# Moving half of the conditioning steps out of the top-16 search into the expert loop and the feed-forward part

## The chip, the core and the metric

The kernel runs on one core of a Trainium2 chip. The core has five engines that each run a queue of their own in order: TensorE (PE) for matmuls, VectorE (DVE), ScalarE (ACT), GpSimd (POOL) and SyncE (SP), which here only issues transfers. Engines wait for each other through semaphores, and transfers between DRAM and the core's SBUF run on 16 DMA engines beside them. The metric is the device time of one execution in microseconds (us). Three runs of the kernel before gave 2368.1, 2367.86 and 2363.62 us: a median of 2367.86 us.

## The reference, cut to what matters

The program is two blocks one after the other on 512 tokens of width 1024. The first is a gated delta rule with a pooling branch, then a product-key mixture of 16,384 experts (eight heads, top 16 of each). The second block is an attention mixer and a feed-forward part, both modulated by six vectors that depend on nothing but a small input `c`. These six vectors are what the text calls the conditioning.

```python
# first block: experts
q = (xb @ w_query).reshape(t, 8, 2, 128)
scores = jnp.einsum("thpc,hpkc->thpk", q, sk)
s1, i1 = lax.top_k(scores[:, :, 0], 16)
s2, i2 = lax.top_k(scores[:, :, 1], 16)
cand = (s1[..., :, None] + s2[..., None, :]).reshape(t, 8, 256)
top_s, top_pos = lax.top_k(cand, 16)
gate = jax.nn.softmax(top_s, axis=-1)
act = gelu(jnp.einsum("td,thkd->thk", xb, expert_down[idx]))
x = x + jnp.einsum("thk,thkd->td", gate * act, expert_up[idx])
...
# second block
mod_all = jnp.einsum('bd,lde->lbe', silu(c), ada_w) + ada_b[:, None]
sh_m, sc_m, gt_m, sh_f, sc_f, gt_f = jnp.split(mod_all[0], 6, axis=-1)
h = modulate(rms_norm(x, norm_g[0, 0]), sh_m, sc_m)
y = stick_breaking_mixer(h, sb_w_qkv, sb_w_o)
x = x + gt_m * rms_norm(y, norm_g[0, 1])
h = modulate(rms_norm(x, norm_g[0, 2]), sh_f, sc_f)
y = swiglu_ffn(h, ffn_w_in, ffn_w_out)
x = x + gt_f * rms_norm(y, norm_g[0, 3])
```

`sh_f` and `sc_f` are first needed in the second block, after attention; `gt_f` is needed at the very end.

## The kernel before, in words

Every matmul is done as three passes on a high and a low part of both factors (`mm3`, lines 198 to 200), so each weight block goes through `split` (line 170): a load of 512 KB into a tile `raw` (SP, line 178), the high part by ACT (`uh` or `wh`, line 187), the low part by DVE or POOL (`ul` or `wl`, line 188). The tiles `raw` share a ring of four buffers for the whole program. SP issues in the order of the program as it is built, so a load whose buffer is not yet free holds back every transfer that SP has behind it. A scheduler that simulates the program sets each engine's order and gives each tile a fixed buffer; both are settled when the program is built.

The stages follow each other in the profiled execution about so (us from the span's start): first mixer 0 to 230, delta rule to 355, output product to 384, search to 539, decoding of the found indices to 612, gates to 877, a tail of expert-down tiles to 925, expert loop to 1675, attention to 1990, output product and feed-forward part to 2365.

The search (from line 1000): for each of 16 half heads a query product with a weight tile (`query`), scores `S`, and the top 16 by DVE (`top16`, lines 980 to 985); after two half heads the 53 candidates `C` (lines 1031 to 1038). The first token block of 128 is done by a gathered path (its rows fetched by POOL's indirect DMA, line 936); the other three, 384 tokens, do all 16,384 experts densely with gates that are zero for those not chosen. An expert-down tile of 128 experts is 24 matmuls of 384 columns and a gelu by ACT (line 975); an expert-up tile is 18 matmuls of 512 columns (three blocks, two halves, three passes). The first 74 down tiles are computed ahead of the loop as fillers (`fill`) and stored to DRAM (`acts`): `FILL_QUERY` of them in the search, others in the delta rule's later part, the decoding and the gates, and the rest of the 74 after the gates (`self.fill(SPILL)`, line 855). The loop over 128 tiles (variable `n`) takes groups of four, one group loading its four stored activations, the next computing them. It multiplies them by the gates (line 882), splits them into `ah` (883) and `al` (884), loads and splits the up tile, and runs the up product two tiles later (`LOOK`). Six of the eight PSUM banks hold its sums.

The conditioning is a generator, `ada` (line 1149), advanced by `ada_steps`. For each of six vectors: eight steps that load 512 KB of `ada_w` into a `raw` tile (1164), scale it by ACT (1165) and add it by POOL (1167); then one step that takes three more `raw` tiles at once, `row` (the bias, loaded from DRAM), `hi` and `lo` (the two parts of the sum, lines 1173 and 1174), runs four matmuls with a matrix of ones and adds the result to `row` (1180); then one step for the finish (a product on POOL and a sum, or for a gate vector a product and a store to DRAM). Thirty steps run in the delta rule and thirty, two after each half head, in the search.

## Time and profile before

| | |
|---|---|
| median of three runs | 2367.86 us |
| profiled execution | 2367.24 us |
| its span on the core | 2365.4 us (1.84 us lie around it) |
| mean granted TensorE clock | 0.979 of full speed |
| PE, DVE, ACT, POOL busy | 95%, 71%, 40%, 37% |
| DMA | 467.90 MB, mean 198 GB/s |

The busy share is an average over stages with different limits; the table of stages among the rows below is read first, then for one stage what each engine waited for. "A <- B" in a table of waits means that A stood idle until B ended. A wait on SP's queue is the time in which a transfer could not be issued.

### The profile page before, as it was taken

To read this page: it belongs to the slowest core of one execution; us is meant where nothing else is said; L and a number is where in the kernel's file an instruction comes from. 1 tells how busy PE (TensorE), PEld (TensorE's weight loads), DVE (VectorE), ACT (ScalarE), POOL (GpSimd) and SP (SyncE) were. 2 spreads that over 40 slices of the span, in tenths; PEclk is the share of its full clock that TensorE was granted. 3 is DMA by queue.
4 is the path that set the end of the run, shared out by engine and by line. 5 is a ranking of instruction groups with operands and counts; after the bars stand their busy time and mean duration, and the time that the engine had idled before them with its cause. 6 is when DMAs were issued, how large, how long until landed. Compare 5 with 4: busy or idle time off the path is not lost.

```text
span 2365.4 us, 31745 instructions
## 1 busy us (share of the span) xinstructions
PE 2245.3 (95%) x11953; PEld 1911.1 (81%) x11953; DVE 1668.4 (71%) x2761; ACT 955.0 (40%) x1422; POOL 885.7 (37%) x553
## 2 busy tenths in 40 slices
PE   7898998887999999999999999999899999999998
PEld 6678767777999999888888888888787667888887
DVE  6675536899999975777878888888747766333334
ACT  4454325444344443433333333333446665322222
POOL 4367414773122112655555656565213331000000
PEclk9899999998999999999999999999999999999999
DMA  4223214455789878899999999999231122322221
GB/s 169 80 73 128 76 63 152 163 196 176 249 321 318 310 276 284 308 316 322 327 320 334 333 323 320 324 323 318 97 99 45 45 83 91 120 98 90 92 85 63
DMA packets 179850, 467.90 MB, mean 198 GB/s; under 512 B 15344, under 2 KB 83952, under 8 KB 178032
## 3 DMA queue, kind: packets, MB, share of 16 engines
q1 hardware_dynamic: 141824, 329.33, 40.4%
q0 software_dynamic: 36864, 134.23, 16.0%
q10 hardware_dynamic: 1008, 2.31, 0.3%
q8 instruction: 93, 1.52, 0.3%
q14 instruction: 61, 0.50, 0.1%
HBM read 420.86 MB, written 44.96 MB: 197 GB/s over the span
## 4 chain that ended last, share of the span: by engine, by line
PE 67%; DVE 14%; DMA 7%; issue 5%; ACT 4%; POOL 3%; SPq 0%; DVEq 0%; ACTq 0%; POOLq 0%
PE bank L198 19%; PE bank L200 19%; PE bank L199 19%; PE bank L1364 3%; PE bank L1137 3%; PE bank L653 3%; DMA act<-acts 2%; DMA raw<-in_e_down_dram 2%; DVE ul L188 2%; DVE su L949 1%; DVE cy L470 1%; DMA raw<-in_ada_w_dram 1%; ACT uh L187 1%; DVE x L955 1%; POOL ada_acc L1167 1%
## 5 line engine op out<-in xcount | busy, mean ns | idle before, releaser
L198 PE MATMUL bank<-actT_h,wh 128*128 128x384 f32 (+2 forms) x1672 | 597.4, 358 | 23.9 <-ACT wh L187 12.2
L200 PE MATMUL bank<-actT_h,wl 128*128 128x384 f32 (+2 forms) x1672 | 587.7, 354 | 14.2 <-POOL wl L188 10.5
L199 PE MATMUL bank<-actT_l,wh 128*128 128x384 f32 (+2 forms) x1672 | 590.0, 353 | 1.6 <-DVE actT_l L331 1.2
L187 ACT ACTIVATE wh<-raw 128x1024 fp32r<-128x1024 f32 x190 | 201.1, 1059 | 418.3 <-PE bank L199 261.5
L198 PEld LDWEIGHTS bank<-actT_h,wh 128*128 128x128 f32 x1672 | 318.2, 190 | 52.3 <-ACT wh L187 15.8
L200 PEld LDWEIGHTS bank<-actT_h,wl 128*128 128x128 f32 x1672 | 317.4, 190 | 40.3 <-POOL wl L188 13.8
L199 PEld LDWEIGHTS bank<-actT_l,wh 128*128 128x128 f32 x1672 | 318.0, 190 | 25.2 <-DVE actT_l L331 1.4
L187 ACT ACTIVATE uh<-raw 128x1024 fp32r<-128x1024 f32 x194 | 202.8, 1052 | 301.1 <-PE bank L200 150.9
L199 PE MATMUL bank<-ul,ah 128*128 128x512 f32 x768 | 303.3, 395 | 0.0
L198 PE MATMUL bank<-uh,ah 128*128 128x512 f32 x768 | 303.0, 395 | 0.0
L200 PE MATMUL bank<-uh,al 128*128 128x512 f32 x768 | 302.0, 395 | 0.8 <-DVE al L884 0.8
L188 POOL TENSOR_TENSOR wl<-raw,wh 128x1024 fp32r<-128x1024 f32 x89 | 224.6, 2525 | 163.6 <-ACT wh L187 79.9
L188 DVE TENSOR_TENSOR ul<-raw,uh 128x1024 fp32r<-128x1024 f32 x167 | 225.9, 1356 | 78.3 <-ACT uh L187 77.6
L936 POOL DMA_INDIRECT su<-in_e_up_dram,rows_of x128 | 191.2, 1493 | 174.1 <-DVE x L955 152.4
L188 DVE TENSOR_TENSOR wl<-raw,wh 128x1024 fp32r<-128x1024 f32 x115 | 140.4, 1222 | 112.6 <-ACT wh L187 111.3
L260 POOL TENSOR_TENSOR rs<-ms,nhalf 128x1 f32<-128x1 f32 (+1 forms) x23 | 16.0, 696 | 458.9 <-DVE ms L259 458.9
L955 DVE SCALAR_TENSOR_TENSOR x<-su,own_act,x 128x1024 f32<-128x1024 f32 x128 | 178.4, 1394 | 1.1
L200 PEld LDWEIGHTS bank<-uh,al 128*128 128x128 f32 x768 | 144.2, 188 | 36.1 <-DVE al L884 1.5
L199 PEld LDWEIGHTS bank<-ul,ah 128*128 128x128 f32 x768 | 144.2, 188 | 32.7
L198 PEld LDWEIGHTS bank<-uh,ah 128*128 128x128 f32 x768 | 144.2, 188 | 32.2
L936 POOL DMA_INDIRECT su<-in_e_rows_dram,rows_of x76 | 110.5, 1454 | 128.1 <-DVE su L949 74.5
L882 DVE TENSOR_TENSOR act<-act,G 128x384 f32<-128x384 f32 x128 | 89.9, 715 | 67.3 <-DMA act<-acts 40.2
(397 smaller groups left out, 3834.2 us busy)
## 6 DMA issues: line engine op xcount, KB each, us to landing
raw<-in_e_down_dram SPq DMA_DIRECT2D x128, 512.0 KB
raw<-in_e_up_dram SPq DMA_DIRECT2D x128, 512.0 KB
raw<-in_ada_w_dram SPq DMA_DIRECT2D x48, 512.0 KB
gates<-stg SPq DMA_DIRECT2D x12, 2048.0 KB
G<-gates SPq DMA_DIRECT2D x32, 768.0 KB
raw<-in_f_in_dram SPq DMA_DIRECT2D x44, 512.0 KB
acts<-act SPq DMA_DIRECT2D x74, 192.0 KB
act<-acts SPq DMA_DIRECT2D x74, 192.0 KB
```

Source lines behind the costliest of these rows:

```text
L187: nc.scalar.activation(hi, raw, AF.Copy)
L188: (lo_engine or nc.vector).tensor_sub(lo, raw, hi.bitcast(F32))
L198: nc.tensor.matmul(ps, l[0], r[0], start=start, stop=False)
L199: nc.tensor.matmul(ps, l[0], r[1], start=False, stop=False)
L200: nc.tensor.matmul(ps, l[1], r[0], start=False, stop=stop)
L470: nc.vector.scalar_tensor_tensor(y, cv[:, i:i + ST], convw[:, 4 * ct + i:4 * ct + i + 1], y, op0=OP.mult, op1=OP.add)
L653: nc.tensor.matmul(ps[:, h * P:(h + 1) * P], l(h), r(h), start=True, stop=True)
L882: nc.vector.tensor_tensor(av, av, G[:, :, j % 4, :], op=OP.mult)
L936: nc.gpsimd.indirect_dma_start(out=t, out_offset=None, in_=down if n < P else up, in_offset=bass.IndirectOffsetOnAxis(ap=self.rows_of[:, n ...
L955: nc.vector.scalar_tensor_tensor(x0, t, act[:, c:c + 1], x0, op0=OP.mult, op1=OP.add)
L1137: nc.tensor.matmul(ps[:, t * P:(t + 1) * P], A[:, 2 * j + t // 2, :, t % 2], B[:, k, 2 * j + t // 2, :, t % 2], start=k == 0, stop=k == 2)
L1364: self.nc.tensor.matmul(o, l, r, start=start, stop=stop, skip_group_check=True)
```

## The change

`FILL_QUERY` sums to 11 where it summed to 6, so five more down tiles are computed between the search's start and its end, and five fewer after the gates. The conditioning no longer runs in the search. The generator yields once more in each vector, between making `lo` and the matmuls with ones, so a vector has 11 steps: 33 are done in the delta rule (the same three vectors), 22 in the expert loop, one at every fourth tile from `n` = 2 to 86 (`sh_f` and `sc_f`), and 11 in the feed-forward part, three at a time (`gt_f`). `gt_f` gets a tile of its own for `row`, which stays in SBUF, without the store to DRAM and the load. In attention a constant matrix of minus ones is made in another way.

```diff
-FILL_QUERY = [0, 1, 0, 1, 0, 1, 0, 3]
+FILL_QUERY = [0, 1, 1, 1, 1, 1, 1, 5]
...
-ADA_DELTA = 30
+ADA_DELTA = 33
...
-                self.sparse_pool = pm, ("su",), 6
+                self.sparse_pool, self.ada_pool = (pm, ("su",), 6), pm
...
                     if n < len(tiles):
                         j = tiles[n]
+                        if n % 4 == 2 and n < 88:
+                            self.ada_steps(1)
...
-            queries, self.ada_pool = {}, pk
+            queries = {}
...
                         self.top16(pk, V[:, T, c, :], I[:, T, c, :], S[:, T, :], P)
-                    self.ada_steps(2)
                 self.fill(FILL_QUERY[h])
...
-            row = raw_tile()
+            row = raw_tile() if name != "gt_f" else self.t(self.ada_pool, [P, D], tag="gate")
             nc.sync.dma_start(row, d["rows"][3 + seg:4 + seg, :].to_broadcast([P, D]))
             hi, lo = raw_tile(F32R), raw_tile(F32R)
             nc.scalar.activation(hi, acc, AF.Copy)
             nc.gpsimd.tensor_tensor(lo, acc, hi.bitcast(F32), op=OP.subtract)
+            yield
             for dh in range(2):
...
-                self.mod[name] = self.t(self.dp, [P, D], tag=name)
-                nc.sync.dma_start(self.mod[name], row)
+                self.mod[name] = row
+                if name == "gt_m":
+                    self.mod[name] = self.t(self.dp, [P, D], tag=name)
+                    nc.sync.dma_start(self.mod[name], row)
...
-            gate = self.t(pz, [P, D], tag="gate")
-            nc.sync.dma_start(gate, self.mod["gt_f"])
+            self.ada_pool = pz
...
                     ws.append(self.split(d["f_out"][f], "u"))
+                self.ada_steps(3)
...
             self.tap("y2", y)
+            gate = self.mod["gt_f"]
```

First place, SP's queue in the search, from the third query load on. In the kernel before (names are tile<-source):

```order
L178 DMA raw_2886<-in_w_query_dram 128x1024
L1164 DMA raw_2950<-in_ada_w_dram 128x1024
L1164 DMA raw_2954<-in_ada_w_dram 128x1024
L178 DMA raw_2958<-in_w_query_dram 128x1024
L1164 DMA raw_3022<-in_ada_w_dram 128x1024
L1164 DMA raw_3026<-in_ada_w_dram 128x1024
L178 DMA raw_3030<-in_w_query_dram 128x1024
```

In the changed kernel at the same place:

```order
L178 DMA raw_2878<-in_w_query_dram 128x1024
L178 DMA raw_2942<-in_w_query_dram 128x1024
L178 DMA raw_3006<-in_w_query_dram 128x1024
L178 DMA raw_3070<-in_e_down_dram 128x1024
L178 DMA raw_3160<-in_w_query_dram 128x1024
L178 DMA raw_3224<-in_w_query_dram 128x1024
L178 DMA raw_3288<-in_e_down_dram 128x1024
```

The loads of `ada_w` between the query loads are gone, and a down tile stands behind every second query.

Second place, SP's queue at the end of the gates, from the last store of the gates on. In the kernel before:

```order
L1146 DMA gates_2761<-stg_8210 128x4096
L178 DMA raw_8642<-in_e_down_dram 128x1024
L844 DMA acts_2762<-act_8496 128x384
L178 DMA raw_8676<-in_e_down_dram 128x1024
L873 DMA G_8787<-gates_2761 128x12x128
L873 DMA G_9019<-gates_2761 128x12x128
L844 DMA acts_2762<-act_8537 128x384
L178 DMA raw_8710<-in_e_down_dram 128x1024
L844 DMA acts_2762<-act_8571 128x384
L178 DMA raw_8744<-in_e_down_dram 128x1024
L844 DMA acts_2762<-act_8605 128x384
L178 DMA raw_8789<-in_e_down_dram 128x1024
```

In the changed kernel:

```order
L1147 DMA gates_2761<-stg_8230 128x4096
L178 DMA raw_8677<-in_e_up_dram 128x1024
L844 DMA acts_2762<-act_8516 128x384
L178 DMA raw_8686<-in_e_down_dram 128x1024
L875 DMA G_8637<-gates_2761 128x12x128
L875 DMA G_8873<-gates_2761 128x12x128
L844 DMA acts_2762<-act_8557 128x384
L178 DMA raw_8724<-in_e_up_dram 128x1024
L1165 DMA raw_8737<-in_ada_w_dram 128x1024
```

Five of the down tiles that stood behind the store are gone; the first up tile is loaded right behind it, and the first block of `ada_w` soon after.

Third place, SP's queue in the loop where the first moved vector reaches its step with `row`, `hi` and `lo`. The kernel before, at the same up tiles:

```order
L178 DMA raw_10494<-in_e_up_dram 128x1024
L178 DMA raw_10528<-in_e_up_dram 128x1024
L178 DMA raw_10560<-in_e_down_dram 128x1024
L876 DMA act_10413<-acts_2762 128x384
L876 DMA act_10450<-acts_2762 128x384
L876 DMA act_10487<-acts_2762 128x384
L873 DMA G_10558<-gates_2761 128x12x128
L876 DMA act_10521<-acts_2762 128x384
L178 DMA raw_10598<-in_e_up_dram 128x1024
L178 DMA raw_10628<-in_e_down_dram 128x1024
```

The changed kernel:

```order
L1172 DMA raw_10369<-in_rows_dram 128x1024
L178 DMA raw_10382<-in_e_up_dram 128x1024
L878 DMA act_10295<-acts_2762 128x384
L878 DMA act_10332<-acts_2762 128x384
L878 DMA act_10375<-acts_2762 128x384
L875 DMA G_10446<-gates_2761 128x12x128
L878 DMA act_10409<-acts_2762 128x384
L178 DMA raw_10416<-in_e_up_dram 128x1024
L875 DMA G_10725<-gates_2761 128x12x128
L178 DMA raw_10448<-in_e_down_dram 128x1024
L178 DMA raw_10486<-in_e_up_dram 128x1024
L178 DMA raw_10516<-in_e_down_dram 128x1024
```

The load of `row` (`raw_10369`) now stands between the 34th and the 35th up tile, and on ACT `hi` (`raw_10371`) and on POOL `lo` (`raw_10372`) are made there too, in two more buffers of the ring. In the built program the buffers of the ring are `raw_10369` in the fourth, `raw_10371` in the first, `raw_10372` in the second, and the seven weight tiles from `raw_10382` on (four up, three down: the five shown, an up tile and a down tile) all in the third; the up tile after them is in the first again. The matmuls that free `hi` and `lo` stand on PE behind the first passes of the down tile that is loaded into `raw_10516`:

```order
L198 MATMUL bank_10522<-actT_h_2532,wh_10518 128x384
L199 MATMUL bank_10522<-actT_l_2533,wh_10518 128x384
L1180 MATMUL bank_10581<-raw_10371,ones_r_1295 128x512
L1181 MATMUL bank_10581<-raw_10372,ones_r_1295 128x512
L198 MATMUL bank_8631<-uh_10488,ah_10481 128x512
```

For the second moved vector (from the 78th up tile) the same happens with four weight tiles in one buffer.

## Rows read from the trace of the kernel before

**Rows 1.** The page: the span and the busy time of each engine (its share of the span, and the number of instructions).

```profile
span 2365.4 us, 31745 instructions
PE 2245.3 (95%) x11953; PEld 1911.1 (81%) x11953; DVE 1668.4 (71%) x2761; ACT 955.0 (40%) x1422; POOL 885.7 (37%) x553
```

**Rows 2.** Busy time of each engine by stage: the search to its last score, the rest of the search, decoding, gates, the tail of down tiles, the expert loop, the feed-forward part. The columns are in the first line.

```profile
core 0: us, PE busy (x) PEld busy (x) DVE busy (x) ACT busy (x) POOL busy (x), PEclk, DMA share, GB/s
384.00:515.00 131.00, 113.56 (x562) 94.24 (x560) 112.74 (x672) 66.20 (x79) 101.93 (x43) 0.97 0.53 178
515.00:539.00 24.00, 15.76 (x76) 13.91 (x75) 24.00 (x146) 8.71 (x11) 9.46 (x4) 0.90 0.52 183
539.00:612.00 73.00, 60.12 (x313) 59.24 (x314) 66.78 (x127) 26.13 (x42) 18.75 (x9) 0.87 0.59 197
612.00:877.00 265.00, 265.00 (x2272) 256.72 (x2271) 247.27 (x371) 120.39 (x190) 55.99 (x44) 1.00 0.85 301
877.00:925.00 48.00, 45.74 (x262) 45.05 (x261) 17.32 (x13) 17.36 (x25) 14.16 (x9) 1.00 0.90 324
925.00:1640.00 715.00, 712.07 (x3355) 611.98 (x3353) 590.96 (x645) 256.52 (x343) 414.76 (x244) 1.00 0.91 320
2000.00:2300.00 300.00, 299.49 (x1353) 246.97 (x1352) 114.51 (x129) 83.72 (x104) 0.00 (x0) 1.00 0.31 102
```

**Rows 3.** ScalarE in the tail after the gates, its activations in order of time: start, duration, line, tile, and in brackets the idle time before and what ended it (the first and the third gelu of three tiles that follow each other, the wait for a load, the first gated activation split for the loop).

```profile
885.03 0.47 ACT L975 ACTIVATE act<-bank 128x384 f32<-128x384 f32 x1
...
893.35 0.47 ACT L975 ACTIVATE act<-bank 128x384 f32<-128x384 f32 x1
...
905.52 1.06 ACT L187 ACTIVATE wh<-raw 128x1024 fp32r<-128x1024 f32 x1 [7.53 <-DMA raw<-in_e_down_dram]
...
922.04 0.50 ACT L883 ACTIVATE ah<-act 128x384 fp32r<-128x384 f32 x1
```

**Rows 4.** The chain that ended last, from the end of the gates into the loop: start, duration, what.

```profile
896.50 8.91 DMA raw<-in_e_down_dram
...
924.81 0.24 PE bank L198
925.04 0.23 PE bank L199
```

**Rows 5.** The search and what follows it to 539 us, instructions grouped by line and shape: count, busy us, mean ns of one, idle time before them.

```profile
L1167 POOL TENSOR_TENSOR ada_acc<-ada_acc,raw 128x1024 f32<-128x1024 f32 x21 | 50.3, 2396 | 7.0 <-ACT raw L1165 4.9 <-DMA raw<-in_e_down_dram 1.8
...
L1031 DVE TENSOR_TENSOR C<-V 128x40 f32<-128x40 f32 x4 | 9.6, 2390 | 0.0
...
L1180 DVE TENSOR_TENSOR raw<-raw,bank 128x512 f32<-128x512 f32 x6 | 4.0, 673 | 0.0
...
L1031 DVE TENSOR_TENSOR C<-V 128x128 f32<-128x128 f32 x4 | 3.4, 844 | 0.0
```

**Rows 6.** What the engines waited for from 384 to 515 us: us in total, times, the longest.

```profile
ACT raw L1165 <- DMA raw<-in_ada_w_dram: 18.5, 17, 2.5
DVE V L980 <- ACT S L1019: 18.3, 4, 5.8
...
PE bank L200 <- POOL wl L188: 8.1, 5, 4.4
```

**Rows 7.** The chain that ended last at the search's begin, where a load stands alone in front of its user.

```profile
388.18 3.85 DMA raw<-in_w_query_dram
...
446.73 4.30 DMA raw<-in_w_query_dram
```

**Rows 8.** What SP's queue waited for in the expert loop, 925 to 1640 us.

```profile
SPq L178 <- DVE ul L188: 341.5, 113, 7.1
SPq L178 <- POOL wl L188: 138.6, 43, 5.7
```

**Rows 9.** The expert loop, 925 to 1640 us, grouped by line and shape, columns as in rows 5.

```profile
L188 DVE TENSOR_TENSOR ul<-raw,uh 128x1024 fp32r<-128x1024 f32 x120 | 162.5, 1358 | 23.8 <-ACT uh L187 23.1
...
L187 ACT ACTIVATE uh<-raw 128x1024 fp32r<-128x1024 f32 x121 | 127.3, 1053 | 123.5 <-DMA raw<-in_e_up_dram 65.6 <-PE bank L200 53.1 <-issue 2.9
L188 POOL TENSOR_TENSOR wl<-raw,wh 128x1024 fp32r<-128x1024 f32 x49 | 125.7, 2565 | 43.7 <-ACT wh L187 43.0
```

**Rows 10.** Loads in the loop, SP's queue and then ScalarE: the issue of an up tile and of a down tile, and the activations that read them.

```profile
1126.59 0.33 SPq L178 DMA_DIRECT2D raw<-in_e_up_dram  x1
1128.85 0.33 SPq L178 DMA_DIRECT2D raw<-in_e_down_dram  x1
...
1134.55 1.06 ACT L187 ACTIVATE uh<-raw 128x1024 fp32r<-128x1024 f32 x1 [8.38 <-DMA raw<-in_e_up_dram]
1136.96 1.06 ACT L187 ACTIVATE wh<-raw 128x1024 fp32r<-128x1024 f32 x1 [1.34 <-DMA raw<-in_e_down_dram]
```

**Rows 11.** VectorE and then GpSimd at one place of the loop: a subtraction that lies beside a POOL instruction, and one that does not.

```profile
1205.85 0.55 DVE L882 TENSOR_TENSOR act<-act,G 128x384 f32<-128x384 f32 x1
1207.66 2.45 DVE L884 TENSOR_TENSOR al<-act,ah 128x384 fp32r<-128x384 f32 x1 [1.26 <-ACT ah L883]
...
1207.30 2.40 POOL L188 TENSOR_TENSOR wl<-raw,wh 128x1024 fp32r<-128x1024 f32 x1 [3.20 <-ACT wh L187]
```

**Rows 12.** Two stretches of the loop by engine, columns as in rows 2.

```profile
1050.00:1100.00 50.00, 49.35 (x230) 41.89 (x229) 41.48 (x56) 18.05 (x23) 31.24 (x19) 1.00 0.97 351
...
1150.00:1200.00 50.00, 50.00 (x226) 41.60 (x225) 43.46 (x64) 15.59 (x21) 29.23 (x20) 1.00 1.00 352
```

More of the change, by code (lines that the diff above doesn't have):

```diff
@@ L1286, in attention @@
             v = self.t(pq, [P, NT, D], tag="v2")
-            nones = self.t(pq, [P, P], tag="nones")
-            nc.vector.memset(nones, -1.0)
             identb = self.t(pq, [P, P], BF16, tag="identb")
@@ L1293, in attention @@
             nones_r = self.t(pq, [P, P], F32R, tag="nones_r")
-            nc.vector.tensor_copy(nones_r, nones)
+            nc.vector.tensor_scalar(nones_r, self.ones, -1.0, None, OP.mult)
+            nones = nones_r.bitcast(F32)
             revcum_r = self.t(pq, [P, P], F32R, tag="revcum_r")
```

## The prediction, made before the changed kernel had run

> **What bounds the kernel now.** I read the page first, then the table by stage, then for each stage that the diff touches what its engines waited for. PE is busy 2245.3 of 2365.4 us [rows 1], so what counts is where it is not full. Two such places are near the change. From 384 to 515 us PE has 113.56 of 131 us and DVE 112.74; in the 24 us after the last score DVE is full and PE has 15.76 [rows 2]. The other is small: the tail of down tiles from 877 to 925, where PE is 45.74 of 48 us busy, but with work that could stand elsewhere. In the gates PE is full and in the expert loop it has 712.07 of 715 us, with DMA at 0.91 of its time [rows 2]. The loop is bound by PE, but only just: SP waits to issue a load 113 times for the low part of an up tile and 43 times for that of a down tile [rows 8], so all four buffers of the ring are in use nearly always, and ScalarE waited 65.6 us for up tiles to land and 53.1 us for PE to free a buffer [rows 9]. Sometimes the up tiles are ahead of PE and sometimes they come late.
>
> **What goes.** After the gates five down tiles fewer. Two tiles take 893.35 - 885.03 = 8.32 us [rows 3], one 4.16, five 20.8 us; all of it on PE's path, so I count -20.8.
>
> In the search, 21 additions of 2.4 us leave POOL (50.3 us), and DVE loses six additions, 4.0 us [rows 5]. DVE also gets freer of POOL: a candidate sum of 128x40 takes 2.39 us there while one of 128x128 takes 0.84 [rows 5]. The waits for `ada_w` (18.5 us, ACT) and for scores (18.3 us, DVE) shrink [rows 6]. But PE gets three more down tiles before the last score (six instead of three, order of the fillers) and loses 12 matmuls with ones at the cadence of 925.04 - 924.81 = 0.23 us [rows 4]: 113.56 + 3 x 4.16 - 2.8 = 123.2 us. PE's own work thus allows at most 131 - 123.2 = 7.8 us. I take -7; the ends are 0 (POOL makes the low parts of the fillers and holds the queries back, 8.1 us now [rows 6]) and -14 (clock or DVE help more than counted). After the last score five tiles, 20.8 us, replace three on PE beside 24 us of DVE: 15.76 + 8.3 = 24.1, just covered; cost 0, up to +4 if the decoding's first matmuls queue behind a tile. Decoding and gates I leave as they are, since DVE has 66.78 of 73 us in the one and PE all in the other [rows 2]. Together -27.8 us.
>
> **What comes, in the loop.** Sixteen loads of 512 KB and two of a broadcast row, 9.4 MB; 18 POOL instructions (14 additions, 2 low parts, 2 products), 18 activations, 8 matmuls, 6 DVE instructions.
>
> (1) *The step with `row`, `hi` and `lo`.* It takes three of four ring buffers at once, and now holds them from the 34th up tile until the matmuls with ones, which stand on PE behind three more tiles. Meanwhile seven tiles, four up and three down, pass through the one buffer left, each load issued only when the tile before it is split. An up tile costs L + 1.05 (ACT) + 1.36 (DVE), a down tile L + 1.06 + 2.57 (POOL) [rows 9], L being the load. L is not shown for this situation: 3.85 to 4.30 us where a load stands nearly alone [rows 7], 8.0 us in the loop with others under way (1126.59 to 1134.55) [rows 10]. With one weight load at a time, but gathers, gates and activations beside it, I take 5: 4 x 7.4 + 3 x 8.6 = 55.4 us. PE needs 18 x 0.23 = 4.2 us for an up tile [rows 4] and 4.16 for a down tile, 29.3 us for the seven. The deficit is 26, less what the tiles are ahead of PE. That is 0 where ScalarE waits for loads and 12.6 (three up tiles) where it waits for PE; I take 4, as the first half of the loop shows late loads [rows 10, 12]. Cost +22. Ends: L 3.85 and 12.6 ahead give 47.4 - 29.3 - 12.6 = +5.5; L 8.0 and nothing ahead give 76.4 - 29.3 = +47.
>
> (2) *The same for the second vector*, with two up and two down tiles through one buffer: 2 x 7.4 + 2 x 8.6 - 16.7 = 15.3 us less the lead. In the second half of the loop the ring runs further ahead, so I take +4 (0 to 15).
>
> (3) *The plain steps.* 9.4 MB at the loop's 320 GB/s are 29 us of DMA time; the loop leaves 9% of 715, 64 us [rows 2], but not evenly: one stretch has a DMA share of 0.97 and PE misses 0.65 of its 50 us, another has 1.00 [rows 12]. Ten stretches of 50 us with about 0.5 us each: +5, ends 0 and +29. DVE is no bound here: 18 x (2.45 - 0.55) [rows 11] = 34 us in 124 us of idle time [rows 2]; if that cover were used up it would cost those 34.
>
> A subtraction on DVE took 2.45 us beside a POOL instruction of 2.40 us, an operation of the same shape 0.55 us apart from one [rows 11]. The Trainium skill, in "SBUF — State Buffer", on the shared port pair, says that a DVE instruction with two SBUF inputs and a GpSimd instruction that reads SBUF exclude each other for a whole instruction; the trace agrees here, and by the rule 18 instructions of 2.4 us would take 43 us of the 124, which changes no bound.
>
> (4) *The loop's start.* The down tiles in the tail gave the first up tiles and activations time to land; one load there took 8.91 us and stood on the chain [rows 4], and the loop's first split comes at 922.04 [rows 3]. With 20.8 us less it may be late: +4, ends 0 and 8.9.
>
> **What comes, in the feed-forward part.** Eleven steps in bursts of three. DMA stands at 0.31 and POOL at nothing there [rows 2], but the bursts take ring buffers, and `hi` and `lo` hold two of four for one group. Four matmuls at 0.23 are 0.9; I take +3, ends 0.9 and 15 (six bursts that each wait for a POOL addition of 2.4). **Delta rule**: three steps more, matmuls with ones later and in front of the output product: 0, ends -4 and +4 (a load each way, [rows 7]). The rest (minus ones, `gt_f` kept) is hidden by PE's work.
>
> **Sum.** -27.8 + 22 + 4 + 5 + 4 + 3 = +10.2 us on 2367.24 us, the profiled execution, which lies 0.6 us under the median: 2377 us.
>
> **Rivals.** *A, the ring's lead covers the step.* Loads alone in the ring take 3.85 us, and the up tiles are some 10 us ahead: step (1) costs 8, the second 0, the rest 2: -27.8 + 10 = 2349 us, faster. For it: PE misses only 3 us in 715 now [rows 2]. Against it: the ring is always full, and one buffer does a tile in 7 to 9 us where PE takes 4.2. It decides as soon as the lead at the 34th up tile is over some 10 us with L under 4.5.
>
> *B, the DMA engines are the bound in the loop.* 0.97 and 1.00 of DMA time at 351 and 352 GB/s [rows 12] would be the ceiling, and every added byte shows: 29 in place of 5, so 2367 + 10 + 24 = 2401 us. For it: these stretches; against it: the mean of 320 GB/s, and PE full at a share of 1.00. The Trainium skill, "DMA: Bandwidth & Descriptors", on where its ceiling comes from, puts the limit of a core's HBM traffic at about 358 GB/s; no stretch read here is above it, and by the rule the 9.4 MB cost an estimated 26 us only if the loop sat at the limit all the way.
>
> *C, the search does not get shorter.* The fillers' PE work and their POOL low parts eat what the conditioning frees, and the decoding waits for two tiles: 0 and +4 in place of -7: 2388 us. For it: PE's 123 us against DVE's 109 in that stretch, so the bound moves from DVE to PE.
>
> **How the numbers follow.** Forecast 0.47 (own range 2368 to 2390, some 0.10 of it within the band of no change and 0.03 below), A 0.27 (2342 to 2362), B 0.13, C 0.13. A measurement of this kernel can tell about 0.2%, 4.7 us, from no change: below 2363 counts as faster, above 2372.6 as slower. Faster 0.27 + 0.03 = 0.30; same 0.12, the forecast's 0.10 with 0.02 of C; slower 0.58. The range of 8 in 10 runs from 2347, which leaves out the better half of A's, to 2398, which leaves out most of B.
>
> **What would show it.** In the profile after: the tail between the gates and the first up product about 27 us long, not 48; the last score some 7 us earlier after the search's begin; PE losing some 20 us between the 34th and 40th up tile, with waits for `uh`, `ul`, `wh` and `wl`, while SP waits for the split of the tile just before each load; little of that at the second vector; in the feed-forward part PE still nearly full. Wrong it would be if PE stays at 50 of 50 us through that step (then A), or if its losses are spread over the first 600 us of the loop at a DMA share near 1 (then B).

## The result and the profile after

The changed kernel takes 2387.63 us (median of four runs, 2382.98 to 2393.72) against 2367.39 us (four runs, 2363.62 to 2368.1): the ratio is 1.0085, 95% interval 1.0062 to 1.0107. It is slower by 20 us. The profiled execution was the fastest of the four (2382.98 us, span 2381.2), so the trace shows 15.8 us of these 20.

The time by stage, first. The stages begin and end earlier now, so the cuts differ from those of [rows 2]; the columns are the same: the search to its last score, the rest of it, decoding, gates, the tail, the loop, the feed-forward part.

```profile
core 0: us, PE busy (x) PEld busy (x) DVE busy (x) ACT busy (x) POOL busy (x), PEclk, DMA share, GB/s
384.00:495.00 111.00, 109.54 (x573) 96.67 (x572) 90.57 (x658) 38.67 (x55) 47.46 (x20) 1.00 0.30 102
495.00:520.00 25.00, 22.69 (x129) 22.05 (x128) 24.46 (x133) 13.74 (x18) 7.74 (x4) 1.00 0.38 121
520.00:602.00 82.00, 73.82 (x465) 71.92 (x464) 77.37 (x134) 30.53 (x50) 36.80 (x12) 0.94 0.63 216
602.00:850.00 248.00, 248.00 (x2115) 240.82 (x2114) 230.65 (x344) 111.68 (x176) 51.73 (x40) 1.00 0.86 306
850.00:885.00 35.00, 27.82 (x140) 26.86 (x139) 10.87 (x16) 12.94 (x18) 12.33 (x9) 0.86 0.98 351
885.00:1640.00 755.00, 715.02 (x3289) 607.00 (x3289) 600.45 (x627) 266.56 (x350) 451.05 (x258) 0.98 0.87 308
2010.00:2310.00 300.00, 299.31 (x1369) 247.34 (x1368) 129.14 (x133) 92.50 (x112) 23.73 (x9) 1.00 0.35 116
```

In the search PE is nearly full where it had 113.56 of 131 us, and in the loop PE now misses 40 of 755 us where it missed 3 of 715. The feed-forward part took the steps of `gt_f` without loss.

Two marks cut the span cleanly: the first and the last score of the search (the activations that write `S`) and the first and the last up product of the loop (here one of its passes; the last product, of another pass, starts 0.5 us after it). The columns are the count, the shortest, median and longest in ns, and the start of the first and of the last. The scores, in the kernel before

```profile
L1019 ACT ACTIVATE S<-bank x16: 577/592/602, 387.7 to 515.3; 128x512 f32<-128x512 f32 x16
```

and in the changed one:

```profile
L1021 ACT ACTIVATE S<-bank x16: 589/594/601, 378.1 to 494.9; 128x512 f32<-128x512 f32 x16
```

The up products, before

```profile
L198 PE MATMUL bank<-uh,ah x768: 390/396/475, 924.6 to 1683.0; 128*128 128x512 f32 x192
```

and after:

```profile
L198 PE MATMUL bank<-uh,ah x768: 390/397/793, 884.7 to 1701.5; 128*128 128x512 f32 x192
```

The loop thus went from 924.6 to 1683.5, 758.9 us, and now goes from 884.7 to 1702.0, 817.3 us. It starts 39.9 us earlier and takes 58.4 us more; what follows it takes 679.2 us against 681.9. That is the whole difference of the spans, -39.9 + 58.4 - 2.7.

Between the last score and the first up product a third mark is useful, the products of the gates, before

```profile
L1137 PE MATMUL bank<-B,A x1152: 217/218/308, 606.7 to 875.6; 128*128 128x128 bf16 x192
```

and after:

```profile
L1138 PE MATMUL bank<-B,A x1152: 217/218/308, 579.6 to 848.3; 128*128 128x128 bf16 x192
```

From the last score to the first of them it was 91.4 us and is 84.7. From the last of them to the first up product, the tail, it was 49.0 us and is 36.4.

Where the loop loses, 50 us at a time, columns as above:

```profile
1025.00:1075.00 50.00, 44.74 (x207) 36.94 (x206) 36.84 (x46) 18.12 (x23) 32.19 (x18) 1.00 0.89 320
1075.00:1125.00 50.00, 38.02 (x160) 31.53 (x161) 25.20 (x38) 11.61 (x17) 19.92 (x13) 0.93 0.63 220
1125.00:1175.00 50.00, 43.45 (x189) 36.26 (x188) 37.58 (x47) 15.63 (x21) 22.70 (x15) 0.90 0.75 262
1375.00:1425.00 50.00, 45.20 (x197) 37.81 (x196) 32.31 (x32) 12.43 (x17) 25.64 (x16) 0.93 0.73 248
```

Two holes stand out, around the steps with `row`, `hi` and `lo` (`hi` is made at 1074.8 and at 1370.6 us). In them PE idles, the granted clock falls to a mean of 0.90 and 0.93, and DMA moves less than elsewhere, 220 to 262 GB/s against about 320: everything waits, and nothing is at its limit. The first hole in detail, SP's queue and then ScalarE:

```profile
1079.48 0.33 SPq L178 DMA_DIRECT2D raw<-in_e_up_dram  x1
...
1093.53 0.33 SPq L178 DMA_DIRECT2D raw<-in_e_up_dram  x1
...
1102.61 0.33 SPq L178 DMA_DIRECT2D raw<-in_e_down_dram  x1
1113.02 0.33 SPq L178 DMA_DIRECT2D raw<-in_e_up_dram  x1
1118.85 0.33 SPq L178 DMA_DIRECT2D raw<-in_e_down_dram  x1
1125.88 0.33 SPq L178 DMA_DIRECT2D raw<-in_e_up_dram  x1
1131.71 0.33 SPq L178 DMA_DIRECT2D raw<-in_e_down_dram  x1
```

```profile
1100.27 1.06 ACT L187 ACTIVATE uh<-raw 128x1024 fp32r<-128x1024 f32 x1 [3.98 <-DMA raw<-in_e_up_dram]
1109.51 1.06 ACT L187 ACTIVATE wh<-raw 128x1024 fp32r<-128x1024 f32 x1 [8.18 <-DMA raw<-in_e_down_dram]
1116.51 1.06 ACT L187 ACTIVATE uh<-raw 128x1024 fp32r<-128x1024 f32 x1 [5.94 <-DMA raw<-in_e_up_dram]
```

Seven weight tiles follow each other one by one, each issued after the split of the one before. The three loads whose user is shown take 6.7, 6.9 and 3.5 us.

### The profile page after: what moved, and what is told of

Its sections match the earlier page's. It is cut to its first block, busy times and chain, and to the rows that moved or that the text cites. A ratio compares the mean times of both kernels' runs of the same rounds, so it can differ in the third digit from the quotient of the medians.

```text
span 2381.2 us, 31688 instructions
## 1 busy us (share of the span) xinstructions
PE 2248.9 (94%) x11953; PEld 1912.6 (80%) x11953; DVE 1674.1 (70%) x2755; ACT 952.4 (40%) x1422; POOL 912.3 (38%) x558
## 4 chain that ended last, share of the span: by engine, by line
PE 52%; DVE 11%; issue 6%; DMA 5%; POOL 3%; ACT 2%; SPq 0%; POOLq 0%; DVEq 0%; ACTq 0%
PE bank L198 15%; PE bank L199 15%; PE bank L200 15%; PE bank L1368 3%; PE bank L1138 3%; DVE ul L188 2%; DVE x L957 2%; DVE su L951 2%; DMA act<-acts 2%; DMA raw<-in_e_up_dram 1%; POOL wl L188 1%; DVE act L884 1%; DMA raw<-in_e_down_dram 1%; POOL su L938 1%; DVE al L886 1%
## 5 line engine op out<-in xcount | busy, mean ns | idle before, releaser
L188 POOL TENSOR_TENSOR wl<-raw,wh 128x1024 fp32r<-128x1024 f32 x94 | 235.7, 2509 | 228.7 <-ACT wh L187 149.1
L200 PE MATMUL bank<-uh,al 128*128 128x512 f32 x768 | 275.4, 397 | 1.8 <-DVE al L886 1.8
L957 DVE SCALAR_TENSOR_TENSOR x<-su,own_act,x 128x1024 f32<-128x1024 f32 x128 | 193.8, 1514 | 1.2
L1168 POOL TENSOR_TENSOR ada_acc<-ada_acc,raw 128x1024 f32<-128x1024 f32 x42 | 105.6, 2514 | 145.4 <-ACT raw L1166 144.0
L938 POOL DMA_INDIRECT su<-in_e_rows_dram,rows_of x76 | 105.1, 1382 | 133.7 <-DVE su L951 77.6
```

Source lines behind the costliest of these rows:

```text
L188: (lo_engine or nc.vector).tensor_sub(lo, raw, hi.bitcast(F32))
L200: nc.tensor.matmul(ps, l[1], r[0], start=False, stop=stop)
L938: nc.gpsimd.indirect_dma_start(out=t, out_offset=None, in_=down if n < P else up, in_offset=bass.IndirectOffsetOnAxis(ap=self.rows_of[:, n ...
L957: nc.vector.scalar_tensor_tensor(x0, t, act[:, c:c + 1], x0, op0=OP.mult, op1=OP.add)
L1168: nc.gpsimd.tensor_tensor(acc, acc, raw, op=OP.add)
```

## The experiments

The ratios are to runs of the kernel before on the same chip (their median was 2367.4 to 2371.0 us). "First" and "last" are the starts of the first and last score and up product as read above, in the profiled execution of each; one trace each, so differences of 3 us or so between them are not read. A new build also places the instructions of other stages anew: the five kernels without the steps in the loop (before, fill_only, in_attention, attn_oldfill, delta_all) have loops of 758.9 to 767.0 us.

| kernel | median us | ratio, 95% | first/last score | first/last up product | loop |
|---|---|---|---|---|---|
| before | 2367.39 | | 387.7 / 515.3 | 924.6 / 1683.5 | 758.9 |
| changed | 2387.63 | 1.0062 to 1.0107 | 378.1 / 494.9 | 884.7 / 1702.0 | 817.3 |
| own_bufs | 2358.98 | 0.9942 to 0.9982 | 380.2 / 497.0 | 885.6 / 1677.7 | 792.1 |
| plain_only | 2346.78 | 0.9902 to 0.9946 | 374.5 / 491.3 | 879.6 / 1660.1 | 780.5 |
| loads_only | 2335.61 | 0.9833 to 0.9886 | 377.5 / 494.3 | 882.9 / 1653.6 | 770.7 |
| adds_only | 2350.15 | 0.9892 to 0.9946 | 379.0 / 495.9 | 890.0 / 1676.4 | 786.4 |
| fill_only | 2376.17 | 1.0024 to 1.0087 | 388.4 / 532.0 | 929.0 / 1691.3 | 762.3 |
| ada_only | 2388.31 | 1.0061 to 1.0113 | 381.2 / 484.5 | 888.4 / 1703.6 | 815.2 |
| in_attention | 2356.03 | 0.9928 to 0.9969 | 379.6 / 496.4 | 883.4 / 1650.4 | 767.0 |
| attn_oldfill | 2358.12 | 0.9940 to 0.9973 | 379.2 / 482.5 | 887.5 / 1652.0 | 764.5 |
| no_yield | 2378.69 | 1.0023 to 1.0060 | 392.7 / 509.5 | 898.3 / 1691.6 | 793.3 |
| own_dve | 2352.04 | 0.9901 to 0.9953 | 375.0 / 491.8 | 882.1 / 1658.3 | 776.2 |
| own_late | 2352.07 | 0.9901 to 0.9940 | 377.1 / 494.0 | 882.4 / 1659.9 | 777.5 |
| delta_all | 2373.99 | 1.0002 to 1.0030 | 414.5 / 531.4 | 919.0 / 1682.4 | 763.4 |

**own_bufs.** The three tiles of the step out of the ring.

```diff
-            row = raw_tile() if name != "gt_f" else self.t(self.ada_pool, [P, D], tag="gate")
+            own = lambda tag, dt=F32: self.t(self.ada_pool, [P, D], dt, tag=tag, bufs=1)
+            row = raw_tile() if seg < 3 else own("gate")
...
-            hi, lo = raw_tile(F32R), raw_tile(F32R)
+            hi, lo = (own("ahi", F32R), own("alo", F32R)) if 3 <= seg < 5 else (raw_tile(F32R), raw_tile(F32R))
```

> The changed kernel, but in the expert loop `row`, `hi` and `lo` of the two moved vectors lie in three tiles of their own and not in the ring of four; loads, additions, matmuls and their places stay. Theory (the step that takes three of four ring buffers starves PE): most of what PE loses around the two steps comes back, 23.8 us of idle time and some 8 us of lower clock between 1025 and 1175 us and about half of that between 1325 and 1425; 2345 to 2355 us, PE near 50 of 50 us in those stretches. Rival (the added bytes and POOL additions cost it all along the loop): under 10 us come back, 2378 us or more.

2358.98 us: 28.6 us come back, and the loop is 25.2 us shorter. It is faster than both kernels. The three stretches from 1075 to 1175 and from 1375 to 1425 us, to be held against the rows of the changed kernel above:

```profile
1075.00:1125.00 50.00, 49.45 (x234) 42.69 (x233) 46.12 (x56) 19.18 (x26) 34.30 (x20) 0.99 0.91 323
1125.00:1175.00 50.00, 50.00 (x228) 41.87 (x227) 40.20 (x63) 17.47 (x23) 26.47 (x19) 1.00 0.97 341
1375.00:1425.00 50.00, 50.00 (x228) 41.75 (x227) 45.15 (x50) 16.65 (x22) 25.29 (x16) 1.00 0.93 317
```

Both holes are gone, while the loads and additions are all still there. The theory holds for 25 of the 58 us; the time expected was a little too low, since the loop still takes 33 us more than before.

**plain_only.** The step left out in the loop, the loads, scalings and additions kept.

```diff
+            if 3 <= seg < 5:
+                yield
+                yield
+                c = self.t(cp, [P, KT], tag=name)
+                nc.vector.tensor_copy(c, acc[:, 0:KT])
+                self.mod[name] = c
+                yield
+                continue
             gate = name[0] == "g"
```

> The changed kernel without the step with `row`, `hi` and `lo` for the two vectors in the loop (and without their finish); the sixteen loads of `ada_w`, scalings and additions stay. This leaves out work: `sh_f` and `sc_f` are not formed. Theory: the loop, from the first up matmul to the last, then takes 765 to 775 us, against 817 in the changed kernel and 759 before, and the run 2340 to 2350. Rival (plain steps): the loop stays over 795 us and the run over 2365.

2346.78 us, as expected for the run; the loop of 780.5 us is some 6 us over. Against fill_only's 762.3 us, which has the same five tiles fewer in its tail, the plain steps cost 18 us, and against in_attention's 767.0 us 13.5. Either is much more than the 5 us of the prediction.

**fill_only.** The kernel before with the new list.

```diff
-FILL_QUERY = [0, 1, 0, 1, 0, 1, 0, 3]
+FILL_QUERY = [0, 1, 1, 1, 1, 1, 1, 5]
```

> The kernel before with the new FILL_QUERY alone; the conditioning stays in the search. If the five tiles fit beside the search: the first up matmul comes 15 to 20 us earlier and the loop takes 759 to 765 us as before: 2348 to 2355 us. Rival (the search is then bound by PE and by POOL's low parts and gives the gain back): within 5 us of 2367. A second rival (the tail was the time in which the first tiles of the loop landed, so a shorter tail costs in the loop): first up matmul 20 us earlier, loop over 770 us.

2376.17 us, slower by 0.24 to 0.87%: the first rival, and more than it said. The search grows from 127.6 to 143.6 us, and from the last score to the first up product it is 397.0 us instead of 409.3. So 16 us are paid for 12, and the loop takes 3.4 us more.

**ada_only.** The changed kernel with the old list (the diff above the other way round).

> The changed kernel with the old FILL_QUERY: the conditioning moves and no filler does. Theory (loss in the loop by the step that holds three buffers): loop 800 to 820 us, some 45 to 60 over before; search some 10 to 15 us shorter; the tail as before, so 2395 to 2410 us. Rival (the loop's loss comes from starting earlier with less loaded): loop under 785 us and the run under 2380.

2388.31 us, within a microsecond of the changed kernel; the search is 103.3 us long, 24.3 less than before, and the loop takes 815 us. The loss in the loop does not need the shorter tail, which rules out the rival. The run was below what I expected because the conditioning alone frees more in the search than I had counted.

**in_attention** and **attn_oldfill.** The 22 steps in attention, with the new list and with the old one.

```diff
-                        if n % 4 == 2 and n < 88:
-                            self.ada_steps(1)
...
             units = [(c, u) for c in range(KT) for u in self.UNITS]
+            self.ada_pool = pq
...
+                if n < 22:
+                    self.ada_steps(1)
                 if n >= len(units) - 3 - LEAD0:
```

> The changed kernel with the 22 steps of `sh_f` and `sc_f` not in the expert loop but in attention, one after each of its first 22 units; the fillers as in the changed kernel. If nothing but the steps made the loop longer: first up matmul at 885 us as in the changed kernel, loop 760 to 765 us as with the fillers alone, and what follows 679 to 690: 2328 to 2342 us. Rival (attention, where DVE is busy 168 of 275 us, cannot hide them, the step with three ring buffers above all): what follows the loop takes over 700 us, 2350 us or more.

> The same, steps in attention, with the old FILL_QUERY, so that no filler moves. If the five fillers only change places (they lengthen the search by what they shorten the tail): within 6 us of the run above, search near 103 us and tail some 14 us longer. If the prediction's term of -20.8 us for the fillers were right by itself: 15 us or more slower than the run above.

2356.03 and 2358.12 us. The loop is 767.0 and 764.5 us, as expected, but what follows it takes 704 us instead of 680: the rival was right about attention. From the loop's end to the last product of attention:

```profile
1684.00:1961.00 277.00, 262.56 (x1260) 196.20 (x1260) 171.77 (x234) 164.19 (x286) 80.44 (x61) 0.98 0.21 71
```

in the kernel before, and with the steps in it

```profile
1650.00:1944.00 294.00, 269.48 (x1279) 200.33 (x1277) 194.98 (x244) 181.05 (x307) 128.05 (x79) 0.97 0.30 99
```

PE idles 24.5 us there instead of 14.4, DVE and ACT have some 23 and 17 us more to do. No engine is full, so the steps probably lengthen a chain; which link of it was not looked into. The two lists differ by 2 us, with a search of 116.8 and 103.3 us: the fillers change places and no more.

**loads_only** and **adds_only** were to split the 18 us of the plain steps.

```diff
                 raw = raw_tile()
                 nc.sync.dma_start(raw, d["ada_w"][seg, k])
+                if 3 <= seg < 5:
+                    nc.scalar.activation(acc[:, 8 * k:8 * k + 8], raw[:, 0:8], AF.Copy, scale=sc[:, k:k + 1])
+                    yield
+                    continue
```

> The changed kernel without the step with `row`, `hi` and `lo` (as in plain_only), and with the sixteen loads of `ada_w` in the loop only: of each loaded block ScalarE reads 8 columns, and GpSimd adds nothing. This leaves out work: `sh_f` and `sc_f` are not formed. If the loads (bytes and ring buffers) make the 18 us by which plain_only's loop is longer than with the fillers alone: loop 776 to 782 us, 2340 to 2350. If ScalarE's and GpSimd's instructions make it: loop under 768 us, 2332 or less.

```diff
+                if 3 <= seg < 5:
+                    raw = self.t(self.ada_pool, [P, D], tag="tmp", bufs=1)
+                    nc.scalar.activation(raw if k else acc, self.xs, AF.Copy, scale=sc[:, k:k + 1])
+                    if k:
+                        nc.gpsimd.tensor_tensor(acc, acc, raw, op=OP.add)
+                    yield
+                    continue
                 raw = raw_tile()
```

> The changed kernel without the step with `row`, `hi` and `lo`, and with the sixteen scalings on ScalarE and fourteen additions on GpSimd in the loop, but on data that lies in SBUF anyway and with a tile of their own, so without the loads and without ring buffers. This leaves out work: `sh_f` and `sc_f` are not formed. If the instructions make the 18 us: loop 776 to 782 us. If the loads make them: loop under 768 us.

2335.61 us with the loads alone and 2350.15 with the instructions alone. With the loads alone the loop is 770.7 us, between the two expectations: 8.4 MB more to load cost some 8 us over fill_only (4 over in_attention), and the scalings and additions of plain_only another 10 (780.5 us; 11 by the medians).

adds_only does not price the instructions where they stand. Without loads and ring buffers nothing held the fourteen additions back, and all of them ran between 867.0 and 967.1 us, four of them before the first up product, where plain_only has them spread from 890.9 to 1325.3:

```profile
L1168 POOL TENSOR_TENSOR ada_acc<-ada_acc,tmp x14: 2350/2402/3380, 867.0 to 964.7; 128x1024 f32<-128x1024 f32 x14
```

Its profiled execution was also its slowest run, 10 us over its median, so its loop of 786 us reads too high.

What the additions do to VectorE shows between loads_only and plain_only, the whole loop of each, columns as above:

```profile
882.90:1653.60 770.70, 762.96 (x3559) 653.96 (x3558) 625.68 (x682) 278.28 (x384) 420.26 (x253) 0.99 0.89 317
```

```profile
879.60:1660.10 780.50, 763.42 (x3559) 652.10 (x3558) 642.53 (x682) 290.49 (x385) 462.47 (x268) 0.99 0.89 313
```

VectorE has 682 instructions in either, and takes 16.9 us longer for them where GpSimd adds beside it. PE idles 17.1 us instead of 7.7.

**no_yield.** The step as in the kernel before, matmuls at once after `lo`.

```diff
             nc.gpsimd.tensor_tensor(lo, acc, hi.bitcast(F32), op=OP.subtract)
-            yield
             for dh in range(2):
...
-ADA_DELTA = 33
+ADA_DELTA = 30
...
-                        if n % 4 == 2 and n < 88:
+                        if n % 4 == 2 and n < 80:
```

> The changed kernel without the added step: in each vector the matmuls with ones follow the making of `lo` at once, as in the kernel before (10 steps a vector, 30 in the delta rule, 20 in the loop). `row`, `hi` and `lo` still come from the ring of four, but in the built program `hi` and `lo` are given back before the 36th up tile's load, so that one weight tile instead of seven passes through a single buffer. Theory (how long three of four buffers are held costs the 25 us between the changed kernel and own_bufs): 2352 to 2365 us, loop 785 to 800. Rival (it is the three tiles' being in the ring at all, or the wait of PE for `lo`, that costs): 2378 or more.

The loop is 793.3 us, as the theory had it and as with own_bufs: it is how long three of four buffers are held that costs. The run is 2378.69 us, as the rival had it, for another reason: the first score comes at 392.7 us instead of 378.1, and what follows the loop takes 691 us instead of 679. The first of these is visible in what PE waited for from 200 to 420 us (`o` is the delta rule's output, `raw` here `hi`), in no_yield

```profile
PE bank L789 <- DVE o L785: 7.4, 2, 5.7
PE bank L1179 <- ACT raw L1174: 7.3, 1, 7.3
```

and in the changed kernel

```profile
PE bank L1180 <- ACT raw L1174: 4.2, 1, 4.2
PE bank L789 <- DVE o L785: 3.0, 2, 2.0
```

With the added step PE waits 3.1 us less for `hi` and 4.4 less for `o`, some 7 of the 14 us; the granted clock is higher too, 0.97 instead of 0.91 from 200 to 378 us. The same step makes the hole in the loop. The 12 us after the loop stand in own_dve, own_late and delta_all too, where 691 to 694 us follow the loop. About 10 of them lie between 220 and 330 us behind the loop's end, in the later part of attention and the output product, which none of the edits touches; the cause was not followed up.

**own_dve.** own_bufs with the additions and `lo` of the loop on VectorE.

```diff
-                    nc.gpsimd.tensor_tensor(acc, acc, raw, op=OP.add)
+                    (nc.vector if 3 <= seg < 5 else nc.gpsimd).tensor_tensor(acc, acc, raw, op=OP.add)
...
-            nc.gpsimd.tensor_tensor(lo, acc, hi.bitcast(F32), op=OP.subtract)
+            (nc.vector if 3 <= seg < 5 else nc.gpsimd).tensor_tensor(lo, acc, hi.bitcast(F32), op=OP.subtract)
```

> own_bufs (`row`, `hi`, `lo` in tiles of their own), with the fourteen additions and the two low parts of the vectors in the loop on VectorE instead of GpSimd. If GpSimd's instructions cost by holding VectorE up (1.9 us each beside a subtraction) and by standing in front of the low parts of down tiles: loop 770 to 782 us against 792 in own_bufs, 2340 to 2350 us. Rival (VectorE, busy 83% of the loop, is what is short, whoever adds): loop 790 us or more, 2357 or more.

The loop is 776.2 us, 16 us shorter than own_bufs' and as expected. The run, 2352.04 us, is only 7 us shorter and 2 over what was expected, since 693.0 us follow the loop instead of 679.4. The loop and what PE waited for in it, in own_bufs

```profile
885.60:1677.70 792.10, 769.67 (x3567) 655.75 (x3565) 652.32 (x685) 291.97 (x387) 478.70 (x272) 0.99 0.88 309
```

```profile
PE bank L198 <- ACT ah L885: 10.9, 7, 3.7
PE bank L200 <- POOL wl L188: 7.9, 7, 2.5
PE bank L200 <- DVE al L886: 2.0, 2, 1.6
```

and in own_dve:

```profile
882.10:1658.30 776.20, 764.30 (x3567) 654.26 (x3565) 642.63 (x701) 293.12 (x386) 440.81 (x255) 0.99 0.90 315
```

```profile
PE bank L200 <- POOL wl L188: 5.8, 5, 1.9
PE bank L198 <- ACT ah L885: 2.9, 3, 1.3
```

VectorE has 16 instructions more, additions of 1.22 us each as a rule and the two low parts, some 21 us together. Yet it is busy 9.7 us less, so its other instructions take some 31 us less. PE's idle time goes from 22.4 to 11.9 us, and most of that is the wait for `ah`, the high part of the gated activation, which ScalarE makes after VectorE's product `act`. GpSimd's low parts `wl`, which the additions also stand before, account for 2 us of it.

**own_late.** own_dve with the steps in the later two thirds.

```diff
-                        if n % 4 == 2 and n < 88:
+                        if n % 4 == 2 and n > 40:
```

> own_dve (tiles of their own, additions on VectorE) with the 22 steps in the loop's last two thirds, at every fourth tile from `n` = 42 to 126 instead of 2 to 86. Theory (a step costs where the up tiles are hardly ahead of PE, which is the loop's first third): loop 762 to 770 us against 775 in own_dve, 2340 to 2348 us. Rival (a step costs the same anywhere in the loop): loop 773 to 780, 2350 to 2356 us. It is also the version with the best chance to be the fastest of all.

2352.07 us and a loop of 777.5: no difference from own_dve. The rival holds for these steps, with tiles of their own and their additions on VectorE: forty tiles later they cost the same, and how far the tiles are ahead of PE there does not decide. For the step that holds ring buffers it was not tried.

**delta_all.** All 55 steps in the delta rule.

```diff
-                    self.ada_steps(1)
+                    self.ada_steps(2 if n <= 22 else 1)
```

with the steps in the loop taken out as in in_attention.

> The changed kernel with the 22 steps of `sh_f` and `sc_f` in the delta rule too: two steps at each of its first 22 turns and one at the next 11, 55 in all; fillers as in the changed kernel. If the delta rule hides them (GpSimd is busy 41 of its 125 us, VectorE 67): first score at 378 to 395 us, the rest as in in_attention up to the loop's end and as before after it: 2330 to 2345 us. Rival (PE, busy 120 of 125 us there, waits for the chain of the delta rule behind them, or for the ring): first score after 410 us, 2358 us or more.

2373.99 us: the first score comes at 414.5 us, 36 us later than in the changed kernel, so the rival was right. From 200 to 420 us PE waited 12.0 us for the delta rule's `o` and 7.5 for `hi`:

```profile
PE bank L789 <- DVE o L785: 12.0, 3, 7.1
PE bank L1178 <- ACT raw L1172: 7.5, 2, 5.0
```

## Why the prediction was right, and where its terms were not

Direction and main cause were right; 2377 us was 10 us under the median, inside the range. That it came so near is in part luck: the loop cost 23 us more than its terms, and the stages ahead of it and behind it gave 18 us more. By its terms, with the trace's numbers in their place:

| term | predicted us | measured us |
|---|---|---|
| delta rule and output product, up to the first score | 0 | -9.6 |
| search, first to last score | -7 | -10.8 |
| rest of the search and decoding (last score to first product of the gates) | 0 | -6.7 |
| five tiles out of the tail (last product of the gates to first up product) | -20.8 | -12.6 |
| loop: three of four buffers held | +22 and +4 | +25.2 (own_bufs) |
| loop: plain steps | +5 | +18 (plain_only against fill_only) |
| loop: start after a shorter tail | +4 | +3.4 (fill_only) |
| loop: the step itself, buffers aside | none | +11.6 (own_bufs against plain_only) |
| after the loop | +3 | -2.7 |

- **The step with `row`, `hi` and `lo`** was right in mechanism and near in size. The seven tiles came one by one, and L, taken as 5, was 3.5 to 6.9 us in the loads shown. The clock was not counted: from 1075 to 1175 and 1375 to 1425 us PE idles 23.3 us, and it has half the clock (1.2 of 2.4 GHz) for 23.9 us, of which it is busy 19.4, so about 10 us more by estimate; the first such stretch, at 1110.8 us, follows 4.7 us in which PE stood. That makes about 33 us, 25 in the first hole and 8 in the second. own_bufs gives back only 25.2 of them, so about 8 are lost again in other places, and that the term agrees with the run within a microsecond is luck. The first up tile in the hole also waited 7 us for VectorE, which made its low part at 1092.29 us, while ScalarE had begun the high part at 1085.23: products of the gathered path stand before it in VectorE's order.
- **The plain steps** are the term in the loop that was mis-sized. The prediction bounded them by DMA, from 0 to 29 us, and let VectorE's 124 us of idle time cover the 34 us by which GpSimd holds it up. They cost 18 us, some 8 with the loads alone and 10 for the instructions, and own_dve's loop is 16 us shorter with additions and low parts off GpSimd. Idle time was no cover: VectorE is busy 82% of own_bufs' loop, and PE waits 10.9 us there for `ah`, which depends on VectorE's product. The rule cited from the Trainium skill ("SBUF — State Buffer", the shared port pair) agrees with the 16.9 us longer that the same 682 VectorE instructions take; the sentence that it changes no bound was wrong. That the port is the reason was not tested by itself.
- **The step itself** was counted at nothing once its buffers were paid for. own_bufs still loses 11.6 us over plain_only. Its two low parts and finishing products on GpSimd are of the kind that own_dve shows to be dear, but own_dve moved additions and low parts together, so the share of each stays open.
- **The gain ahead of the loop** was 39.9 us and not 27.8, and its split was wrong. The failed term is -20.8, which took the five tiles' PE time out of the tail whole. The tail became 12.6 us shorter, and PE waits in it now, 4.4 us for `wh` and 2.8 for `wl`, at a mean granted clock of 0.86 (1.00 before): the late start that the prediction put at +4 in the loop lies here, 8 us of it. Another 6.7 us came from the stretch before the gates, which the prediction left as it was; ada_only has 5.4 of them without a filler.
- **The fillers** by themselves are worth nothing that can be told (2387.6 and 2388.3 us; 2356.0 and 2358.1 in attention). With the conditioning out, the new list lengthens the search by 13.5 us (103.3 to 116.8) and shortens the way from the last score to the loop by 14.1 (403.9 to 389.8). The gain is the conditioning's leaving, 24 to 27 us in the search alone, and the added step in the delta rule. The prediction's sum for the search did hold both, with 7.8 us as the most that PE allowed; 10.8 came, and the 113.56 us of PE's time that it started from were taken at a mean granted clock of 0.97, where the changed search has 1.00.
- **The delta rule** was taken as 0 with ends of -4 and +4; the first score comes about 10 us earlier with the added step (378 against 388 and 393 us in the kernels without it).
- Rival A fell: the lead did not cover the step. Rival B fell: with the loads alone the loop is 8 us longer and not 29. Rival C fell too, since the search is 10.8 us shorter, but its bound was real: PE is at 109.54 of 111 us there.

## What to carry to other kernels

A step that takes several tiles of a ring at once and holds them until a later matmul turns the ring into a single buffer for whoever shares it; give such tiles buffers of their own, or issue the matmul before the next load (either gave the loop 24 to 25 us back here). Moving an instruction from one engine's idle time to another's is not free when the two engines hold each other up: here the additions cost less on VectorE itself than on GpSimd beside it. And a filler that leaves one place must be priced in the place it goes to, on the stretch as it will be and not as it was.

## What was not expected of the hardware

With the additions and low parts on GpSimd (2.59 us each on the mean) the loop was 792 us, with the same instructions on VectorE (1.22 us each as a rule) 776, although VectorE was the busier engine, about 83% before. Loads of 512 KB with no other weight load under way took 3.5 to 6.9 us in the same 40 us of the loop. And adding 8.4 MB of loads to a loop that moved 320 GB/s cost about 8 us, where their bytes at that rate are 26.
